# Dense products of a two-block model on one core: one plain fp32 matmul in place of three fp32r matmuls of high and low parts

## The chip, the cores and the metric

One Trainium2 chip, of which the kernel uses one core. The time is microseconds on the device for one execution. Three runs of the kernel before gave 1518.33, 1518.96 and 1520.04 us, a median of 1518.96.

## What is computed

256 tokens of width 1024 go through two blocks in float32. Block 1 has a mixer (gated linear attention beside retention) and a mixture of 32 experts with two experts a token. Block 2 has two layers: a gated recurrence, then a feed-forward; latent attention, then a second feed-forward. Cut to the dense products, it is:

```python
proj = u @ w_in                                   # 1024 -> 11280, split into q, k, v and gates
y_a, y_b = o_gla @ w_br_gla, o_ret @ w_br_ret
h = h + (sigmoid(mga) * y_a + sigmoid(mgb) * y_b) @ w_out
h = h + moe(rmsnorm(h))                           # 32 experts, 1024 -> 512 -> 1024
h = h + hgrn(rmsnorm(h))                          # 1024 -> 4096, recurrence, 1024 -> 1024
h = h + ffn(rmsnorm(h))                           # 1024 -> 2 x 2816, 3-tap convolution, 2816 -> 1024
h = h + mla(rmsnorm(h))                           # 1024 -> 576 latents -> q, k, v; softmax; 1024 -> 1024
h = h + ffn(rmsnorm(h))
```

All weights are float32, 353 pieces of at most 1 MB each.

## The kernel before

Activations stand feature-major (features on partitions, 256 tokens along the free axis) where they are the operand of a product, and token-major elsewhere. Weights come in slots: tiles of 128 x 2048 float32 in a pool of NS = 20, which large activations share. One ordered stream of loads runs on SP's queue (_load, line 302). plan_loads (line 190) goes through a dry run of the program, counts live slots, and so fixes at which points (prefetch) the next loads are issued; a load then waits on SP until its slot's last readers are done, and everything later on SP waits behind it.

A weight other than an expert's is not used as loaded. _split_to (line 311) makes two more slots of it, in four parts each: ACT copies the slot to the format fp32r (high part, tile wh, line 324), and DVE subtracts that from the weight (low part, tile wl, line 325). It runs one weight ahead of the product, two in parts of the attention. Activations are split as well: after a transpose, high_low (line 458) writes xh on ACT and xl on DVE; a feed-forward's hidden tile g is split into hh and hl.

Each product of the dense layers then is three fp32r matmuls (mm3, lines 357 to 361):

```python
mm(out, lh, rh, start=first, stop=False)
mm(out, lh, rl, start=False, stop=False)
mm(out, ll, rh, start=False, stop=last)
```

Names on TensorE: gf is gemm_feat (a weight's 128 x 128 tile stands in the array, 256 tokens stream by), gt is gemm_tok (128 x 128 of the activation stands, 512 weight columns stream by, 288 in the attention's first product), op is out_proj, br the retention branch's product, u and acc the feed-forward's two products (256 and 512 columns), gd a 16-feature product. The experts (gu, y, cb, xg), the retention core (rs, ro), the recurrences' scores (sc, sd, o) and the attention's scores use plain fp32 matmuls on float32 tiles, before and after.

Between the dense products, tick() puts pieces of side work (fillers: decay levels on DVE, scores on TensorE, evacuations on ACT) into the program. The decay levels (tile lv, line 541) are a chain on DVE of eight steps of three operations. In a feed-forward two hidden tiles (u) are followed by the second product (acc) of an earlier pair of them.

Of the kernel before, what the change touches and what calls it, by code (L numbers as in the profile page):

```python
# [12 lines left out]
F32R = mybir.dt.float32r  # L13
# [6 lines left out]
P = 128  # L20
# [10 lines left out]
# 1 / 10000 ** linspace(0, 1, 128) and 10000 ** (-arange(0, 64, 2) / 64), in float32 as the reference rounds them  # L31
# [17 lines left out]
# ---------------------------------------------------------------- host: constants of the shapes  # L49
# [32 lines left out]
# ---------------------------------------------------------------- host: layout of the inputs  # L82
# [79 lines left out]
NS = 20  # L162
# [3 lines left out]
class _Null:  # L166
    """Stands in for the chip while the life of the tiles is counted."""
# [22 lines left out]
def plan_loads(events):  # L190
    """The points of the program at which each weight slot is loaded: as early as the slots allow."""
# [31 lines left out]
class Kern:  # L223
    BUFS = {"t512": 5, "t384": 3, "t256": 7, "t128": 7}

    def __init__(self, ctx, tc, A, coff, poff, upto=None):
# [19 lines left out]
        self.spl = {}  # L246
        self.nsplit = 0
        self.ahead = 1
# [3 lines left out]
    # ---- tiles  # L252
# [37 lines left out]
    # ---- weights: one ordered stream of slots  # L290
    def add(self, key, ap, split):
        self.pos[key] = len(self.stream)
        self.stream.append((key, ap, split))
# [8 lines left out]
    def _load(self):  # L302
        key, ap, split = self.stream[self.loaded]
        t = self.S("w")
        w = ap.shape[-1]
        self.nc.sync.dma_start(t[:, :w], ap)
        self.raw[key] = (t, w)
        self.loaded += 1
        self.events.append("L")

    def _split_to(self, i):
        while self.nsplit <= i and self.nsplit < len(self.stream):
            key, ap, split = self.stream[self.nsplit]
            if not split:
                break
            if self.loaded <= self.nsplit:
                self._load()
            r, w = self.raw.pop(key)
# [7 lines left out]
            self.free(r)  # L326
            self.spl[key] = (h, l)
            self.nsplit += 1

    def get(self, key):  # L330
        i = self.pos[key]
        if self.stream[i][2]:
            self._split_to(i + self.ahead)
            self.prefetch()
            return self.spl.pop(key)
        while self.loaded <= i:
            self._load()
        self.nsplit = max(self.nsplit, i + 1)
        self.prefetch()
        return self.raw.pop(key)[0]  # L340

    # ---- work that runs beside the main products
# [13 lines left out]
    # ---- products  # L356
    def mm3(self, out, lh, ll, rh, rl, first, last):
        mm = self.nc.tensor.matmul
        mm(out, lh, rh, start=first, stop=False)  # L359
        mm(out, lh, rl, start=False, stop=False)  # L360
        mm(out, ll, rh, start=False, stop=last)  # L361

    def gemm_tok(self, keys, xs, evac, kk=4, n=512, ticks=0):
        """[tokens, n] = x @ W; xs(k) -> (high, low, column of the k tile)."""
# [3 lines left out]
        for key in keys:  # L368
            h, l = self.get(key)
            for q in range(kk):  # L370
                xh, xl, o = xs(k)
                for t in range(2):
                    a = slice(o + t * P, o + (t + 1) * P)
                    self.mm3(outs[t][:, :n], xh[:, a], xl[:, a], h[:, q * n:(q + 1) * n], l[:, q * n:(q + 1) * n],
                             k == 0, k == nk - 1)
                k += 1
                if q < kk - 1:
                    self.tick((q + 1) * ticks // kk - q * ticks // kk)
            self.free(h, l)
            self.tick(ticks - (kk - 1) * ticks // kk)  # L380
        evac(outs)

    def gemm_feat(self, keys, xs, evac, kk=4, ticks=0):
        """[512 features, tokens] = W.T @ x.T, two feature tiles a bank."""
# [3 lines left out]
        for key in keys:  # L388
            h, l = self.get(key)
            for q in range(kk):  # L390
                xh, xl, o = xs(k)
                a = slice(o, o + T)
                for ft in range(4):
                    b = slice(q * 512 + ft * P, q * 512 + (ft + 1) * P)
                    self.mm3(outs[ft // 2][:, (ft % 2) * T:(ft % 2 + 1) * T], h[:, b], l[:, b], xh[:, a], xl[:, a],
                             k == 0 and ft % 2 == 0, k == nk - 1 and ft % 2 == 1)
# [3 lines left out]
            self.free(h, l)  # L400
# [3 lines left out]
    def out_proj(self, name, xs, done, mid=None, ticks=0):  # L404
        """x += a @ W, by halves of k, so that the second half of a may come late; done(c): chunk c of x is final."""
        outs = [[self.bank("op") for _ in range(2)] for _ in range(2)]
        for kh in range(2):
            if kh and mid:
                mid()
            for c in range(2):  # L410
                h, l = self.get((name, 2 * kh + c))
                for q in range(4):
                    xh, xl, o = xs(4 * kh + q)
                    for t in range(2):
                        a = slice(o + t * P, o + (t + 1) * P)
                        w = slice(q * 512, (q + 1) * 512)
                        self.mm3(outs[c][t], xh[:, a], xl[:, a], h[:, w], l[:, w], kh == 0 and q == 0,
                                 kh == 1 and q == 3)
                self.free(h, l)
# [7 lines left out]
    # ---- normalisation  # L427
# [22 lines left out]
    def norm_open(self, full=False):  # L450
        n = {"ss": self.small(4, "nss"), "sq": []}
        if full:
            n["f"] = self.S("xf")
        else:
            n["h"], n["l"] = self.S("xh", F32R), self.S("xl", F32R)
        return n

    def high_low(self, b, s, h, l, o):
        a = slice(o, o + T)
        self.nc.scalar.activation(h[:, a], b[:, :T], AF.Copy, scale=s)  # L460
        if l is not None:
            self.nc.vector.scalar_tensor_tensor(l[:, a], b[:, :T], s, h[:, a].bitcast(F32), op0=ALU.mult,
                                                op1=ALU.subtract)

    def norm_chunk(self, n, c, src, wcol):
        """Columns 512 c.. of src [tokens]: transposed, times the weight, split; and their square sums."""
        nc = self.nc
        for k in range(4 * c, 4 * c + 4):
# [3 lines left out]
            self.high_low(b, wcol(k), n.get("h", n.get("f")), n.get("l"), k * T)  # L472
# [18 lines left out]
    def row_of(self, rs):  # L491
        """[128, 256]: the tokens' factors along the free axis, on every partition."""
# [8 lines left out]
    def xs(self, n):  # L501
        return lambda k: (n["h"], n["l"], k * T)

    def transpose_hl(self, src, nk, scale, dst):
        """src(k, t) -> [128 tok, 128]; scale(k) -> [128, 1]; dst(k) -> (high, low, column)."""
        for k in range(nk):
# [3 lines left out]
            self.high_low(b, scale(k), *dst(k))  # L510
# [14 lines left out]
    def decay_levels(self, fr, kq, lv):  # L525
        """[128, 512 + 512] (2 heads x 256 tokens, feature-major) each: products behind | decays (used up); k | q."""
# [23 lines left out]
    def decay_scores(self, lv, kq, h):  # L550
        """Score tiles of one head: SBUF [128, 384] = S^T(0,0) | S^T(0,1) | S^T(1,1)."""
# [42 lines left out]
    def decay_out(self, lv, kq, v, h0, dv):  # L594
        """Both heads of a group: rmsnorm of the output (its weight comes later) in place of v."""
# [44 lines left out]
    # ---------------------------------------------------------------- the program  # L640
# [5 lines left out]
    def setup(self):  # L646
# [14 lines left out]
        for i in range(44):  # L661
            self.add(("in", i), A["w_in"][i], True)
        for n, order in (("br_gla", range(4)), ("br_ret", (0, 4, 1, 5, 2, 6, 3, 7)), ("w_out", range(4))):
            for i in order:
                self.add((n, i), A[n][i], True)
        for e in range(NE):
            for i in range(4):
                self.add(("gu", e, i), A["ex_gu"][e, i], False)
            for i in range(2):
                self.add(("ed", e, i), A["ex_d"][e, i], False)  # L670
        for n, m in (("hg_in", 16), ("hg_out", 4)):
            for i in range(m):
                self.add((n, i), A[n][i], True)

        def ffn(l):
            for kind, i in self.ffn_order():
                if kind == "up":
                    self.add(("f_up", l, i), A["f_up"][l * 22 + i], True)
                else:
                    self.add(("f_dn", l, i), A["f_dn"][l * 11 + i], True)  # L680

        ffn(0)
        for n, o, m in (("ml_in", 0, 4), ("ml_kv", 0, 2), ("ml_q", 0, 3), ("ml_kv", 2, 2), ("ml_out", 0, 4)):
            for i in range(o, o + m):
                self.add((n, i), A[n][i], True)
        ffn(1)

    def slack(self, phase):
        """Slots that the loads leave free for what the phase itself needs next."""
        self.events.append(("slack", SLACK.get(phase, 2)))  # L690

    # ---- block 1, mixer
    def block1_mixer(self):
# [52 lines left out]
        gh, gl = self.small(128, "t128", F32R), self.small(128, "t128", F32R)  # L746
        self.pin(nc.scalar.copy(gh, wgd))
        nc.vector.tensor_sub(gl, wgd, gh.bitcast(F32))
# [970 lines left out]
```

## Time and profile before

| | |
|---|---|
| runs | 1518.33, 1518.96, 1520.04 us |
| profiled execution, first to last instruction (span) | 1516.6 us |
| instructions in it | 24847 |
| bytes read from HBM | 367.24 MB |
| mean granted TensorE clock, share of full | 0.986 |
| weight loads | 353, of 1024 KB or less |

The profiled execution's own time is known as its span; the median of the three runs lies 2.4 us above it. PE stands for TensorE's matmuls, PEld for its weight loads, DVE for VectorE, ACT for ScalarE, POOL for GpSimd and SP for the engine that issues the loads. The length that the trace gives for a matmul contains its way through the array, so consecutive matmuls overlap; the distance between two starts is what one takes of the engine. A busy share of PE is therefore read beside the starts. The granted clock has two levels, 2.4 GHz and 1.2 GHz, shown as 1.00 and 0.50 of full; a mean in between says how long the lower one was given.

### The profile page before, as it was taken

The numbers are of one execution on the slowest core, as the hardware profiler recorded it, in microseconds if no ns is written. First come the engines' busy times: TensorE is split into PE (matmuls) and PEld (weight loads), VectorE is DVE, ScalarE is ACT, GpSimd is POOL, SyncE is SP. The second block draws the span as 40 slices with busy tenths as digits, with TensorE's granted clock in tenths as the row PEclk, the third lists the DMA queues.
The fourth block names the chain that finished last, engine by engine and source line by source line (L and its number), as shares of the span: only waits on it lengthen the run. The fifth ranks groups of instructions, "written<-read, shape, count | busy, mean of one in ns | idle before, by whom it ended". The sixth has DMA issues, their size and how long they took to land. (4 is left out here: it accounts for less than half of the span.)

```text
span 1516.6 us, 24847 instructions
## 1 busy us (share of the span) xinstructions
PE 1435.2 (95%) x10158; PEld 1061.3 (70%) x10158; DVE 792.6 (52%) x1738; ACT 624.9 (41%) x1374; POOL 26.5 (2%) x31
## 2 busy tenths in 40 slices
PE   7999999999899988989989899999999998999998
PEld 7898878877743333333333298779999986799997
DVE  5987475655400000000000079878777767687794
ACT  5645444644200000000000085466656676565672
POOL 0000000000000000000000000000000001000000
PEclk9999999999899999999999999899999999999999
DMA  8335432586799999999999923456554214565500
GB/s 355 130 112 210 179 138 87 201 323 235 295 418 421 421 421 420 420 421 421 421 421 421 408 69 124 152 223 226 191 174 140 72 54 194 200 220 195 192 1 29
DMA packets 53529, 369.96 MB, mean 244 GB/s; under 512 B 6161, under 2 KB 7057, under 8 KB 9634
## 3 DMA queue, kind: packets, MB, share of 16 engines
q1 hardware_dynamic: 53410, 368.31, 62.1%
q8 instruction: 82, 1.34, 0.3%
q14 instruction: 37, 0.30, 0.1%
HBM read 367.24 MB, written 1.05 MB: 243 GB/s over the span
## 5 line engine op out<-in xcount | busy, mean ns | idle before, releaser
L325 DVE TENSOR_TENSOR wl<-w,wh 128x512 fp32r<-128x512 f32 (+2 forms) x644 | 403.9, 666 | 75.1 <-ACT wh L324 56.5
L324 ACT ACTIVATE wh<-w 128x512 fp32r<-128x512 f32 (+2 forms) x644 | 347.8, 613 | 158.6 <-PE u L360 65.8
L1207 PE MATMUL y<-w,t 128*32 128x512 f32 x512 | 227.4, 597 | 10.7 <-ACT t L1200 10.7
L359 PE MATMUL u<-xh,wh 128*128 128x256 f32 x704 | 199.4, 283 | 0.0
L360 PE MATMUL u<-xl,wh 128*128 128x256 f32 x704 | 199.2, 283 | 0.0
L361 PE MATMUL u<-xh,wl 128*128 128x256 f32 x704 | 199.1, 283 | 0.0
L1197 DVE TENSOR_TENSOR t<-t,gu 128x128 f32<-128x128 f32 x32 | 9.2, 288 | 315.5 <-ACT t L1196 315.5
L1207 PEld LDWEIGHTS y<-w,t 128*32 128x32 f32 x512 | 53.9, 110 | 160.7 <-issue 143.3
L1193 PE MATMUL gu<-w,t 128*32 128x256 f32 x2048 | 144.4, 382 | 0.0
L359 PE MATMUL gt<-wh,xh 128*128 128x512 f32 (+1 forms) x352 | 139.4, 396 | 0.0
L359 PEld LDWEIGHTS u<-xh,wh 128*128 128x128 f32 x704 | 134.9, 192 | 0.9
L360 PEld LDWEIGHTS u<-xl,wh 128*128 128x128 f32 x704 | 134.9, 192 | 0.8
L360 PE MATMUL gt<-wl,xh 128*128 128x512 f32 (+1 forms) x352 | 135.2, 384 | 0.0
L361 PE MATMUL gt<-wh,xl 128*128 128x512 f32 (+1 forms) x352 | 135.2, 384 | 0.0
L361 PEld LDWEIGHTS u<-xh,wl 128*128 128x128 f32 x704 | 134.9, 192 | 0.0
L1196 ACT ACTIVATE t<-gu 128x128 f32<-128x128 f32 x32 | 8.9, 278 | 252.2 <-PE gu L1193 252.2
L1193 PEld LDWEIGHTS gu<-w,t 128*32 128x32 f32 x2048 | 68.9, 109 | 56.9 <-issue 20.2
L359 PE MATMUL gf<-xh,wh 128*128 128x256 f32 x320 | 93.4, 292 | 1.7 <-ACT wh L324 1.7
L360 PE MATMUL gf<-xl,wh 128*128 128x256 f32 x320 | 91.9, 287 | 0.0
L361 PE MATMUL gf<-xh,wl 128*128 128x256 f32 x320 | 91.5, 287 | 0.0
L359 PEld LDWEIGHTS gt<-wh,xh 128*128 128x128 f32 x352 | 66.8, 190 | 12.8 <-ACT wh L324 0.5
L360 PEld LDWEIGHTS gt<-wl,xh 128*128 128x128 f32 x352 | 66.8, 190 | 12.9 <-issue 1.0
(394 smaller groups left out, 2144.8 us busy)
## 6 DMA issues: line engine op xcount, KB each, us to landing
w<-in_ex_gu SPq DMA_DIRECT2D x128, 1024.0 KB, 19.0
w<-in_ex_d SPq DMA_DIRECT2D x64, 1024.0 KB, 19.6
w<-in_w_in SPq DMA_DIRECT2D x44, 1024.0 KB, 5.4
w<-in_f_up SPq DMA_DIRECT2D x44, 1024.0 KB, 4.9
w<-in_f_dn SPq DMA_DIRECT2D x22, 1024.0 KB, 4.8
w<-in_hg_in SPq DMA_DIRECT2D x16, 1024.0 KB, 15.7
w<-in_br_ret SPq DMA_DIRECT2D x8, 1024.0 KB, 6.4
w<-in_br_gla SPq DMA_DIRECT2D x4, 1024.0 KB, 5.5
```

The lines of the kernel that those rows point to most:

```text
L324: self.nc.scalar.activation(h[:, a], r[:, a], AF.Copy)
L325: self.nc.vector.tensor_sub(l[:, a], r[:, a], h[:, a].bitcast(F32))
L359: mm(out, lh, rh, start=first, stop=False)
L360: mm(out, lh, rl, start=False, stop=False)
L361: mm(out, ll, rh, start=False, stop=last)
L1193: nc.tensor.matmul(b[32 * j:32 * j + 32, 0:256], xg[k // 4][:, (k % 4) * P + 32 * e:(k % 4) * P + 32 * e + 32], w[:, o:o + 256], start=k = ...
L1196: nc.scalar.activation(sg, b[:, 0:128], AF.Silu)
L1197: nc.vector.tensor_mul(hd, sg, b[:, 128:256])
L1207: self.nc.tensor.matmul(ys[c][32 * e:32 * e + 32, :], hT[:, 32 * j:32 * j + 32], ed[j // 2][:, o:o + 512], start=j == 0, stop=j == 3)
```

## The change

mm3, _split_to and high_low go. Every dense product becomes one plain fp32 matmul on the weight's slot as it was loaded and on one float32 activation tile. A transposed activation is evacuated by one engine (scaled: DVE for odd tiles, ACT for even ones). A weight has one slot instead of two, activations one slot instead of two (xf, oT, rT, mT, cT), and NS is 21. The split of the hidden tile goes, so does the 16-feature weight's. The order of the loads, the experts, the fillers and their ticks stay.

```diff
-NS = 20
+NS = 21
...
-    def _split_to(self, i):
-        while self.nsplit <= i and self.nsplit < len(self.stream):
...
-            h = self.S("wh", F32R)
-            l = self.S("wl", F32R)
-            parts = 4
-            for q in range(parts):
-                a = slice(q * w // parts, (q + 1) * w // parts)
-                self.nc.scalar.activation(h[:, a], r[:, a], AF.Copy)
-                self.nc.vector.tensor_sub(l[:, a], r[:, a], h[:, a].bitcast(F32))
...
     def get(self, key):
...
+        while self.loaded <= self.pos[key]:
             self._load()
         self.prefetch()
+        return self.raw.pop(key)
...
-    def mm3(self, out, lh, ll, rh, rl, first, last):
...
     def gemm_tok(self, keys, xs, evac, kk=4, n=512, ticks=0):
...
-            h, l = self.get(key)
+            w = self.get(key)
             for q in range(kk):
-                xh, xl, o = xs(k)
+                x, o = xs(k)
                 for t in range(2):
-                    a = slice(o + t * P, o + (t + 1) * P)
-                    self.mm3(outs[t][:, :n], xh[:, a], xl[:, a], h[:, q * n:(q + 1) * n], l[:, q * n:(q + 1) * n],
-                             k == 0, k == nk - 1)
+                    self.nc.tensor.matmul(outs[t][:, :n], x[:, o + t * P:o + (t + 1) * P], w[:, q * n:(q + 1) * n],
+                                          start=k == 0, stop=k == nk - 1)
...
-    def high_low(self, b, s, h, l, o):
-        a = slice(o, o + T)
-        self.nc.scalar.activation(h[:, a], b[:, :T], AF.Copy, scale=s)
-        if l is not None:
-            self.nc.vector.scalar_tensor_tensor(l[:, a], b[:, :T], s, h[:, a].bitcast(F32), op0=ALU.mult,
-                                                op1=ALU.subtract)
+    def scaled(self, dst, src, s, k):
+        if k % 2:
+            self.nc.vector.tensor_scalar(dst, src, s, None, op0=ALU.mult)
+        else:
+            self.nc.scalar.activation(dst, src, AF.Copy, scale=s)
...
             for k in range(8):
                 a = slice(k * T, (k + 1) * T)
                 for s in range(2):
-                    w = slice(k * 256 + s * P, k * 256 + (s + 1) * P)
-                    self.mm3(b[:, s * T:(s + 1) * T], h[:, w], lo[:, w], xH[:, a], xL[:, a], k == 0 and s == 0,
-                             k == 7 and s == 1)
+                    nc.tensor.matmul(b[:, s * T:(s + 1) * T], wu[:, k * 256 + s * P:k * 256 + (s + 1) * P], xT[:, a],
+                                     start=k == 0 and s == 0, stop=k == 7 and s == 1)
...
-            nc.scalar.activation(hh, g, AF.Copy)
-            nc.vector.tensor_sub(hl, g, hh.bitcast(F32))
-            hid[f] = (hh, hl)
+            hid[f] = g
```

gemm_feat, out_proj, the retention branch, the feed-forward's second product and the 16-feature product change in the same way.

How instructions stand, at three places. First TensorE in the first feed-forward, where the first hidden tile u begins; before, three matmuls a product, on the high and low parts of the activation and the weight:

```order
L361 MATMUL u_8299<-xh_8199,wl_8222 128x256
L359 MATMUL u_8299<-xh_8199,wh_8221 128x256
L360 MATMUL u_8299<-xl_8200,wh_8221 128x256
L361 MATMUL u_8299<-xh_8199,wl_8222 128x256
L359 MATMUL u_8299<-xh_8199,wh_8221 128x256
L360 MATMUL u_8299<-xl_8200,wh_8221 128x256
L361 MATMUL u_8299<-xh_8199,wl_8222 128x256
L359 MATMUL u_8299<-xh_8199,wh_8221 128x256
L360 MATMUL u_8299<-xl_8200,wh_8221 128x256
```

The same place after, where equal rows follow each other and are counted (x16 is a whole hidden tile):

```order
L1349 MATMUL u_5795<-xf_5744,w_5199 128x256 x15
L451 MATMUL rw_5832<-ident,rsr_5830 128x128 x2
L1349 MATMUL u_5851<-xf_5744,w_5201 128x256 x16
L1349 MATMUL u_5882<-xf_5744,w_5203 128x256 x16
L1376 MATMUL acc_5787<-w_5412,t_1027_5846 128x512
L1376 MATMUL acc_5789<-w_5412,t_1027_5846 128x512
L1376 MATMUL acc_5788<-w_5412,t_1027_5846 128x512
```

Every product now is one instruction; the sequence of u and acc is the same.

Second, DVE in the gated recurrence, at the first decay levels of a group (lv; hfr holds the decays). Before:

```order
L325 TENSOR_TENSOR wl_6700<-w_5914,wh_6699 128x512 x3
L541 TENSOR_TENSOR lv_6716<-hkq_6376,hfr_6375 128x512
L325 TENSOR_TENSOR wl_6748<-w_5916,wh_6747 128x512
L545 TENSOR_TENSOR hfr_6375<-hfr_6375 128x256
L325 TENSOR_TENSOR wl_6748<-w_5916,wh_6747 128x512
L546 TENSOR_TENSOR hfr_6375<-hfr_6375 128x256
L325 TENSOR_TENSOR wl_6748<-w_5916,wh_6747 128x512
L541 TENSOR_TENSOR lv_6716<-hkq_6376,hfr_6375 128x512
```

After:

```order
L1257 TENSOR_TENSOR hkq_4560<-hkq_4560,hfr_4559 128x2x512
L498 TENSOR_TENSOR lv_4708<-hkq_4560,hfr_4559 128x512
L502 TENSOR_TENSOR hfr_4559<-hfr_4559 128x256
L503 TENSOR_TENSOR hfr_4559<-hfr_4559 128x256
L498 TENSOR_TENSOR lv_4708<-hkq_4560,hfr_4559 128x512
```

The weights' subtractions have gone from between the steps of the chain.

Third, ACT in the latent attention, at the evacuation of the keys (kn) from their product's banks. Before:

```order
L1522 COPY kn_10675<-gt_10686 128x512
L1524 ACTIVATE t_1489_10723<-gt_10686 128x512
L1522 COPY kn_10675<-gt_10687 128x512
L1524 ACTIVATE t_1490_10727<-gt_10687 128x512
L324 ACTIVATE wh_10732<-w_10109 128x256 x4
L1522 COPY kn_10675<-gt_10730 128x512
L1524 ACTIVATE t_1495_10755<-gt_10730 128x512
```

After:

```order
L1464 COPY kn_6771<-gt_6782 128x512
L1466 ACTIVATE t_1200_6789<-gt_6782 128x512
L1464 COPY kn_6771<-gt_6783 128x512
L1466 ACTIVATE t_1201_6793<-gt_6783 128x512
L1464 COPY kn_6771<-gt_6796 128x512
L1466 ACTIVATE t_1205_6805<-gt_6796 128x512
```

Here the copies to the high part have gone from between the evacuations.

## Rows read from the trace of the kernel before

**Rows 1.** The page: busy us, share of the span and instructions of each engine.

```profile
PE 1435.2 (95%) x10158; PEld 1061.3 (70%) x10158; DVE 792.6 (52%) x1738; ACT 624.9 (41%) x1374; POOL 26.5 (2%) x31
```

**Rows 2.** Stretches: length; PE, PEld, DVE, ACT, POOL busy (instructions); clock, DMA share, GB/s.

```profile
0.00:380.00 380.00, 368.51 (x2298) 311.94 (x2299) 247.60 (x500) 188.62 (x375) 8.46 (x14) 1.00 0.53 198
380.00:872.00 492.00, 443.56 (x3054) 188.73 (x3052) 45.72 (x161) 41.10 (x113) 0.70 (x1) 0.99 0.99 410
872.00:1026.00 154.00, 145.14 (x1635) 127.90 (x1636) 127.77 (x272) 91.28 (x226) 8.12 (x10) 0.94 0.39 140
1026.00:1222.00 196.00, 195.90 (x1367) 182.61 (x1367) 154.59 (x310) 119.38 (x243) 0.70 (x1) 1.00 0.45 157
1222.00:1326.00 104.00, 95.57 (x506) 75.98 (x504) 70.62 (x207) 74.39 (x203) 7.86 (x4) 0.97 0.41 155
1326.00:1516.60 190.60, 186.52 (x1307) 174.14 (x1306) 146.29 (x292) 110.08 (x218) 0.70 (x1) 1.00 0.37 129
```

**Rows 3.** Timeline of PE, first feed-forward: start us, us, engine, line, operation, tiles.

```profile
1103.72 0.39 PE L359 MATMUL acc<-wh,t 128*128 128x512 f32 x1
...
1107.22 0.28 PE L359 MATMUL u<-xh,wh 128*128 128x256 f32 x1
...
1111.77 0.28 PE L361 MATMUL u<-xh,wl 128*128 128x256 f32 x1
```

**Rows 4.** Timeline of PE in the mixer, at the retention core.

```profile
175.76 1.02 PE L955 MATMUL rs<-rqT,rkT 128*128 128x256 f32 x4
176.62 0.61 PE L958 MATMUL rs<-rqT,rkT 128*128 128x128 f32 x4
...
177.30 0.40 PE L360 MATMUL gt<-wl,xh 128*128 128x512 f32 x1
...
182.10 0.39 PE L360 MATMUL gt<-wl,xh 128*128 128x512 f32 x1
...
182.56 1.02 PE L965 MATMUL ro<-rv,t 128*128 128x512 f32 x2
...
184.28 1.02 PE L967 MATMUL ro<-rv,t 128*128 128x512 f32 x2
```

**Rows 5.** Groups on PE and PEld: tiles, count | busy us, mean ns | idle before.

```profile
L359 PE MATMUL u<-xh,wh 128*128 128x256 f32 x704 | 199.4, 283 | 0.0
L359 PE MATMUL gt<-wh,xh 128*128 128x512 f32 x320 | 129.8, 406 | 0.0
L1217 PE MATMUL cb<-t,t 128*128 128x512 f32 x64 | 29.6, 605 | 0.0
L361 PEld LDWEIGHTS u<-xh,wl 128*128 128x128 f32 x704 | 134.9, 192 | 0.0
```

**Rows 6.** Groups of the split on DVE and ACT, whole span.

```profile
L325 DVE TENSOR_TENSOR wl<-w,wh 128x512 fp32r<-128x512 f32 (+2 forms) x644 | 403.9, 666 | 75.1 <-ACT wh L324 56.5
L324 ACT ACTIVATE wh<-w 128x512 fp32r<-128x512 f32 (+2 forms) x644 | 347.8, 613 | 158.6 <-PE u L360 65.8
```

**Rows 7.** Waits of PE in the mixer, 0 to 380 us: us, times, longest.

```profile
PE gf L359 <- ACT wh L324: 1.7, 1, 1.7
PE gt L360 <- DVE wl L325: 1.2, 1, 1.2
```

**Rows 8.** Waits of PE in the gated recurrence, 872 to 1026 us.

```profile
PE sd L565 <- DVE lv L541: 4.2, 4, 2.1
PE tp L471 <- PEq L1119: 4.1, 1, 4.1
```

**Rows 9.** Groups on DVE in the gated recurrence, 872 to 1026 us.

```profile
L325 DVE TENSOR_TENSOR wl<-w,wh 128x512 fp32r<-128x512 f32 x80 | 52.6, 683 | 1.0 <-ACT wh L324 1.0
```

**Rows 10.** Waits of PE in the latent attention, 1222 to 1326 us.

```profile
PE gt L360 <- DVE wl L325: 3.9, 4, 2.3
PE tp L1553 <- DVE kn L1561: 2.5, 1, 2.5
```

**Rows 11.** Waits of PE in the experts, 380 to 872 us.

```profile
PE gu L1198 <- DMA w<-in_ex_gu: 1.6, 2, 0.8
```

More of the change, by code (lines that the diff above doesn't have):

```diff
@@ L302, in _load @@
     def _load(self):
-        key, ap, split = self.stream[self.loaded]
+        key, ap = self.stream[self.loaded]
         t = self.S("w")
@@ L354, in drain @@
             self.tick()
-    def mm3(self, out, lh, ll, rh, rl, first, last):
[L358 to L361, printed above, removed]
     def gemm_tok(self, keys, xs, evac, kk=4, n=512, ticks=0):
@@ L410, in out_proj @@
             for c in range(2):
-                h, l = self.get((name, 2 * kh + c))
+                w = self.get((name, 2 * kh + c))
                 for q in range(4):
-                    xh, xl, o = xs(4 * kh + q)
+                    xt, o = xs(4 * kh + q)
                     for t in range(2):
[L415 to L419, printed above, removed]
+                        self.nc.tensor.matmul(outs[c][t], xt[:, o + t * P:o + (t + 1) * P],
+                                              w[:, q * 512:(q + 1) * 512], start=kh == 0 and q == 0,
+                                              stop=kh == 1 and q == 3)
+                self.free(w)
                 self.tick(ticks)
@@ L501, in xs, with transposed @@
     def xs(self, n):
-        return lambda k: (n["h"], n["l"], k * T)
-    def transpose_hl(self, src, nk, scale, dst):
+        return lambda k: (n["x"], k * T)
+    def transposed(self, src, nk, scale, dst):
         for k in range(nk):
@@ L751, in block1_mixer @@
             a = slice(k * T, (k + 1) * T)
-            self.mm3(b[0:16, :T], gh[:, k * 16:(k + 1) * 16], gl[:, k * 16:(k + 1) * 16], n["h"][:, a], n["l"][:, a],
-                     k == 0, k == 7)
+            nc.tensor.matmul(b[0:16, :T], wgd[:, k * 16:(k + 1) * 16], n["x"][:, a], start=k == 0, stop=k == 7)
         gd17 = self.small(256, "t256", rows=17)
@@ L906, in block1_mixer @@
         for i in range(2):
-            self.gemm_tok([("br_gla", 2 * i + j) for j in range(2)], lambda k: (oH, oL, k * T), ev_a(i))
-        self.free(oH, oL)
+            self.gemm_tok([("br_gla", 2 * i + j) for j in range(2)], lambda k: (oT, k * T), ev_a(i))
+        self.free(oT)
         outs = [[self.bank("br") for _ in range(2)] for _ in range(2)]
@@ L920, in block1_mixer @@
                     for t in range(2):
-                        a = slice(o + t * P, o + (t + 1) * P)
-                        w = slice(q * 512, (q + 1) * 512)
-                        self.mm3(outs[c][t], xh[:, a], xl[:, a], h[:, w], l[:, w], j == 0 and q == 0,
-                                 j == 3 and q == 3)
-                self.free(h, l)
+                        nc.tensor.matmul(outs[c][t], xr[:, o + t * P:o + (t + 1) * P], w[:, q * 512:(q + 1) * 512],
+                                         start=j == 0 and q == 0, stop=j == 3 and q == 3)
+                self.free(w)
                 if j == 3:
@@ L930, in block1_mixer @@
                         nc.vector.tensor_add(mer[:, a], mer[:, a], mg[1][:, a])
-                    self.now(self.transpose_hl(
+                    self.now(self.transposed(
                         lambda k, t: mer[:, t * D + (4 * c + k) * P:t * D + (4 * c + k + 1) * P], 4, lambda k: 1.0,
-                        lambda k: (mH, mL, (4 * c + k) * T)))
+                        lambda k: (mT, (4 * c + k) * T)))
             if j % 2:
-                self.free(xh, xl)
+                self.free(xr)
         self.free(*mg)
@@ L1431, in down @@
                     for t in range(2):
-                        a = slice(t * P, (t + 1) * P)
                         w = slice(q * 1024 + c * 512, q * 1024 + (c + 1) * 512)
-                        self.mm3(acc[2 * t + c], hs[q][0][:, a], hs[q][1][:, a], h[:, w], lo[:, w],
-                                 i == 0 and q == 0, i == 10 and q == 1)
-            self.free(h, lo)
+                        nc.tensor.matmul(acc[2 * t + c], hs[q][:, t * P:(t + 1) * P], wd[:, w],
+                                         start=i == 0 and q == 0, stop=i == 10 and q == 1)
+            self.free(wd)
         for kind, i in self.ffn_order():
             (up if kind == "up" else down)(i)
-        self.free(xH, xL)
+        self.free(xT)
         nm = self.p("nmix2")
```

156 lines of the change are left out of this document (59 added, 97 removed).

## The prediction

> **What bounds the kernel now.** I read the engines' shares first, then busy time by stretch, then the start times of matmuls, and last the waits. The shares give TensorE (PE) 95% of the span, VectorE (DVE) 52%, ScalarE (ACT) 41% [rows 1]. A busy PE can still be a badly fed one, so the stretches come next [rows 2]. I cut the span at 380, 872, 1026, 1222 and 1326 us: block 1's mixer, the experts, the gated recurrence (HGRN), the first feed-forward, latent attention, the second feed-forward. PE stands idle 0.1 us in the first feed-forward's 196, about 4 in the second's 191 and 11.5 in the mixer's 380. Only HGRN (8.9 idle of 154, mean granted clock 0.94, DVE busy 127.8) and attention (8.4 of 104, clock 0.97) show anything that a relieved DVE or ACT could give back. So the change is decided by what one product costs PE.
>
> A matmul's shown length is no price, since matmuls overlap: u lasts 283 ns [rows 5] but starts every 120 ns. I price by distance of starts. In the feed-forward 38 starts lie between 1107.22 and 1111.77, 120 ns each, and 15 between 1103.72 and 1107.22, 233 ns each at 512 columns [rows 3]; in the mixer 21 starts from 177.30 to 182.10 give 229 ns [rows 4]. Those are the fp32r prices, and each product has three.
>
> Plain fp32 already runs in the same stretch, on 128x128 weights, in the retention core. The trace shows every plain fp32 matmul as two records. Four records of rs (256 columns) take 175.76 to 176.62, 215 ns each; four of ro (512 columns) take 182.56 to 184.28, 430 ns each [rows 4]. The mean of cb, 605 against gt's 406 for the same shape, tells the same of 64 more records [rows 5].
>
> **The change, priced.** Product of 256 columns: 3 x 120 = 359 ns becomes 2 x 215 = 430, +71. Product of 512 columns: 3 x 229 = 686 becomes 2 x 430 = 860, +174; in acc, which pays 233 now, 3 x 233 = 700 becomes 860, +160. For the 32 products of 288 columns I scale the first by width, +80. The clock is at its upper level where I took these.
>
> Products come from the loops of the code, and the counts of the groups agree where they are shown (u 704, gt 320) [rows 5].
> - Mixer: 192 gf and 8 gd of 256 columns, +14.2 us; 256 gt, 32 gt on oh, 64 br and 32 op of 512, 384 in all, +66.8. Together +81.0.
> - Experts: already plain fp32, untouched.
> - HGRN: 128 gf, +9.1; 64 gt and 32 op, +16.7. Together +25.8.
> - Each feed-forward: 352 u, +25.0; 88 acc, +14.1. Both together +78.2.
> - Attention: 28 gt on the latents and 32 op, +10.4; 32 of 288 columns, +2.6. Together +13.0.
>
> All of it is 198 us, if PE is always the last to be ready.
>
> What comes off the other engines: 644 subtractions (403.9 us of DVE) and 644 copies (347.8 us of ACT) [rows 6], half the evacuations of transposed activations (now one engine each, by turns, where before ACT and then DVE did every one), and the split of the hidden tiles. In both feed-forwards that is worth nothing, since PE waits there for neither. Elsewhere I take back only named waits and lost clock:
> - Mixer: the first product's wait for wh, 1.7 us, and one for wl, 1.2 [rows 7]. -3.
> - HGRN: 8.9 us idle, of which 4.1 is the branch behind the experts and stays [rows 8]. Most of the other 4.8 is scores waiting for DVE's decay levels (4.2) [rows 8], and DVE gets 52.6 of its 127.8 us back [rows 2, 9]. The clock of 0.94 costs 0.06 x 154 = 9.2 us, which denser PE work should win back. Together -14. Bounds: nothing back, or all 25.8, as PE then still has that work to do.
> - Attention: the wait for wl, 3.9 us, goes, and the one for kn, 2.5, shrinks with ACT's four-part copies gone from between the evacuations [rows 10]; with some clock (0.03 x 104 = 3 us) I take -8. Bounds 0 and -11.5, all idle time and lost clock.
>
> The remaining edits cost nothing. The loads keep their number and order on SP's queue and gain lead (one slot a weight instead of two behind the split, 21 slots for 20). What hides them is that a 1.05 MB load takes 2.6 us at 410 GB/s [rows 2] and a slot now feeds PE for 6.9 us (16 products of 430 ns, or 8 of 860); without that cover each late load would cost up to 2.6 us. The decay table's load, now behind more weight loads on SP, is first used near 176 us. Nothing moves on POOL. Nothing new waits: a product waits for its load instead of for a split of it.
>
> Sum: mixer 78, HGRN 12, feed-forwards 78, attention 5, which is **+173 us**. The profiled span of 1516.6 becomes 1690; the median of the runs, 1518.96, is 2.4 above that span, so I forecast **1692**.
>
> **A rule weighed against rows.** A group's weight loads last 192 ns in u [rows 5] while u starts every 120 ns [rows 3], so a load runs beside the matmul before it, and the number of loads sets no time. The Trainium skill (TensorE: Matmul & The Clock Gate, part 3, The mechanism) says that a weight load overlaps matmuls in flight only when its row group differs. All dense products here use all rows, so by that rule the loads would stand in line, which is the third rival below. The trace disagrees: a start every 120 ns has no room for a 192 ns load in line. By the row the sum is +173, by the rule it would be a gain.
>
> **The rivals.**
> - *Nothing comes back.* The freed DVE and ACT time is worth nothing because PE's stalls in HGRN and attention are dependencies that merely move. For it: DVE's levels are a chain of steps. Against: its wl subtractions stand between those steps now. +198, **1717**.
> - *Dense plain fp32 has the surplus that fp32r has.* From 120 and 229 ns, an fp32r matmul costs 109 for 256 columns and 11 more, while plain records show 215 and 430 with none [rows 3, 4]. If those 11 ns came from dense switching of weights and not from the format, 1780 x 2 records would pay them too: 39 us on 1692, **1731**. Against: rs switches weights at every record too.
> - *The other side: weight loads set the pace.* Then the drop from three loads a product to two is what counts: 1780 x 192 ns = 342 us gained against 198 lost, **1375**. It decides as soon as over 111 ns of a load (198/1780) stand uncovered. For it: the weight-load row is busy 70% of the span [rows 1]. Against: 192 does not fit into 120.
> - *The expert stage was bound by its loads.* DMA is at 0.99 there [rows 2]. Then five more loads ahead (the four slots of two split weights, and the one added) would save about 5 x 2.6 = 13 us: **1679**. Against: PE waits 1.6 us for those loads in all [rows 11], so the two are only near each other.
> - *The change doesn't do what it says*, a product still being issued as several. The order on PE shows one instruction a product, so this is left only within the chance of no change.
>
> **How the numbers follow.** The forecast has 0.75, for 1672 to 1710 (HGRN from +1 to +26, attention from +1 to +13, the mixer 4 less to 3 more). Nothing back: 0.09. The surplus: 0.06. The expert stage: 0.06, inside the same range. The weight loads: 0.03. No change: 0.01. I take the range from 1665, the forecast's low end with part of the experts' 13 us, to 1722, past the case with nothing back; that leaves out the surplus, the weight loads and the outer ends, under 0.2. About 0.2% (3 us) can be told from no change by a measurement. Faster by more than that is the weight-load case alone, 0.03; within it 0.01; slower 0.96.
>
> **What would show it.** Right: plain u records start every 215 ns and acc and gt every 430; the two feed-forwards take about 39 us more each and are full of PE; the experts keep their 490 us or so; HGRN has a granted clock nearer 1 and fewer waits for lv. Wrong in size: record distances of 226 and 441, or HGRN 25 us longer with its waits in place. Wrong altogether: record distances of about 120 and 230, or a feed-forward shorter than 196 us.

## The result and the profile after

Four runs of the changed kernel gave 1687.62 to 1689.66 us, a median of **1688.67**, beside 1518.64 for the kernel before on the same chip (1518.04 to 1520.04): a ratio of 1.112 [1.1104, 1.1136] (in brackets, here and below, the 95% interval). The forecast was 1692, range 1665 to 1722. Slower came, by 170 us where 173 was forecast.

The page of the changed kernel, busy time of each engine, then the granted clock in 40 slices and three groups:

```profile
PE 1622.0 (96%) x8378; PEld 939.8 (56%) x8378; DVE 409.4 (24%) x1003; ACT 263.8 (16%) x639; POOL 24.1 (1%) x31
...
PEclk9999999999989999999999999999999999999999
...
L1349 PE MATMUL u<-xf,w 128*128 128x256 f32 x1408 | 307.8, 379 | 0.0
...
L1349 PEld LDWEIGHTS u<-xf,w 128*128 128x128 f32 x1408 | 267.1, 190 | 43.7 <-issue 8.6
...
L1376 PE MATMUL acc<-w,t 128*128 128x512 f32 x352 | 154.3, 592 | 0.0
```

Against [rows 1], DVE lost 383 us of work and ACT 361; PE gained 187 and sets the time. There are 1780 matmul records and 1780 weight loads fewer (10158 to 8378), and the kernel is slower. 704 products u show as 1408 records: two a product.

The timeline of PE after, in the second feed-forward (start us, us, engine, line, operation, tiles, count):

```profile
1483.68 13.98 PE L1349 MATMUL u<-xf,w 128*128 128x256 f32 x64
1497.49 7.03 PE L1376 MATMUL acc<-w,t 128*128 128x512 f32 x16
1504.36 1.89 PE L1349 MATMUL u<-xf,w 128*128 128x256 f32 x8
```

64 records of u take 13.81 us, 216 ns each, and 16 of acc 6.87, 429 each, as rs and ro did before [rows 4].

Now the stretches. The prediction's cuts do not fall on the same work in two kernels, so from here on all are cut at work: the mixer ends at the first matmul of the router, the experts with HGRN's first transposes, HGRN at the first u, each feed-forward at its last acc or first u. After (length; PE, PEld, DVE, ACT, POOL busy; clock, DMA share, GB/s):

```profile
0.00:472.00 472.00, 464.57 (x1794) 255.11 (x1795) 108.94 (x250) 59.97 (x126) 7.17 (x14) 1.00 0.47 177
472.00:952.00 480.00, 429.01 (x2993) 177.90 (x2992) 41.83 (x157) 36.53 (x103) 0.70 (x1) 0.98 0.99 410
952.00:1121.70 169.70, 168.68 (x1424) 110.52 (x1423) 81.45 (x185) 46.94 (x136) 7.36 (x10) 0.99 0.41 155
1121.70:1350.00 228.30, 228.30 (x890) 167.93 (x889) 69.30 (x144) 36.82 (x77) 0.69 (x1) 1.00 0.36 123
1350.00:1455.20 105.20, 102.85 (x397) 60.53 (x396) 37.74 (x127) 45.44 (x121) 7.50 (x4) 1.00 0.42 160
```

Before, the three stretches that gave something back, with the same cuts (mixer, HGRN, attention):

```profile
0.00:396.80 396.80, 385.21 (x2378) 325.58 (x2378) 254.03 (x509) 194.36 (x389) 8.46 (x14) 1.00 0.54 203
877.40:1032.10 154.70, 147.85 (x1651) 129.37 (x1649) 131.00 (x278) 94.47 (x233) 8.12 (x10) 0.96 0.38 139
1221.00:1323.30 102.30, 93.87 (x491) 74.19 (x489) 68.90 (x203) 72.08 (x194) 7.86 (x4) 0.97 0.39 150
```

Cut exactly at those matmuls (the table's last row is the price of the products less the measured difference):

| us | mixer | experts | HGRN | 1st feed-forward | attention | 2nd feed-forward |
|---|---|---|---|---|---|---|
| before | 396.8 | 480.6 | 154.7 | 188.9 | 102.3 | 188.9 |
| after | 471.9 | 479.7 | 170.1 | 227.9 | 105.6 | 227.9 |
| difference | +75.1 | -0.9 | +15.4 | +39.0 | +3.3 | +39.0 |
| price of the products | +81.0 | 0 | +25.8 | +39.1 | +13.0 | +39.1 |
| came back | 5.9 | 0.9 | 10.4 | 0.1 | 9.7 | 0.1 |

The waits of PE after: in the mixer (0 to 472 us), then in HGRN (952 to 1122), then in attention (1350 to 1455.2); us, times, longest:

```profile
PE tp L465 <- DVE mga L881: 0.7, 1, 0.7
PE gf L357 <- DVE xf L417: 0.6, 1, 0.6
```

```profile
PE sc L519 <- issue: 0.6, 1, 0.6
PE op L378 <- ACT oT L419: 0.4, 1, 0.4
```

```profile
PE tp L1494 <- DVE rope L1508: 1.3, 1, 1.3
...
PE tp L1494 <- DVE kn L1502: 0.5, 1, 0.5
```

The waits for wl and wh are gone [rows 7, 10], for lv too [rows 8], and kn's fell from 2.5 to 0.5 us. What is new is small: 1.3 us for rope in attention and 0.6 for the first xf.

### The profile page after: what moved, and what is told of

The parts are those of the page before. It is cut to its first block, busy times and chain, and to the rows that moved or that the text cites. A ratio compares the mean times of both kernels' runs of the same rounds, so it can differ in the third digit from the quotient of the medians.

```text
span 1687.8 us, 19722 instructions
## 1 busy us (share of the span) xinstructions
PE 1622.0 (96%) x8378; PEld 939.8 (56%) x8378; DVE 409.4 (24%) x1003; ACT 263.8 (16%) x639; POOL 24.1 (1%) x31
## 5 line engine op out<-in xcount | busy, mean ns | idle before, releaser
L1349 PE MATMUL u<-xf,w 128*128 128x256 f32 x1408 | 307.8, 379 | 0.0
L338 PE MATMUL gt<-w,xf 128*128 128x512 f32 (+1 forms) x704 | 295.7, 575 | 0.0
L1349 PEld LDWEIGHTS u<-xf,w 128*128 128x128 f32 x1408 | 267.1, 190 | 43.7 <-issue 8.6
L338 PEld LDWEIGHTS gt<-w,xf 128*128 128x128 f32 x704 | 131.8, 190 | 143.9 <-issue 137.8
L1376 PE MATMUL acc<-w,t 128*128 128x512 f32 x352 | 154.3, 592 | 0.0
L357 PE MATMUL gf<-xf,w 128*128 128x256 f32 x640 | 144.2, 384 | 0.6 <-DVE xf L417 0.6
L357 PEld LDWEIGHTS gf<-xf,w 128*128 128x128 f32 x640 | 122.0, 193 | 19.3 <-issue 1.8
L1376 PEld LDWEIGHTS acc<-w,t 128*128 128x128 f32 x352 | 66.9, 190 | 75.7 <-issue 68.4
L1362 DVE SCALAR_TENSOR_TENSOR t<-t,prm,t 128x255 f32<-128x255 f32 (+1 forms) x176 | 81.2, 482 | 32.5 <-ACT t L1360 29.4
L378 PE MATMUL op<-w,oT 128*128 128x512 f32 x128 | 56.5, 594 | 0.4 <-ACT oT L419 0.4
```

What stands on the lines that cost most here:

```text
L338: self.nc.tensor.matmul(outs[t][:, :n], x[:, o + t * P:o + (t + 1) * P], w[:, q * n:(q + 1) * n], start=k == 0, stop=k == nk - 1)
L357: self.nc.tensor.matmul(outs[ft // 2][:, (ft % 2) * T:(ft % 2 + 1) * T], w[:, q * 512 + ft * P:q * 512 + (ft + 1) * P], x[:, o:o + T], sta ...
L378: self.nc.tensor.matmul(outs[c][t], xt[:, o + t * P:o + (t + 1) * P], w[:, q * 512:(q + 1) * 512], start=kh == 0 and q == 0, stop=kh == 1 ...
L1349: nc.tensor.matmul(b[:, s * T:(s + 1) * T], wu[:, k * 256 + s * P:k * 256 + (s + 1) * P], xT[:, a], start=k == 0 and s == 0, stop=k == 7 a ...
L1362: nc.vector.scalar_tensor_tensor(ys[:, j:], us[:, :T - j], cw[:, 3 * c + 2 - j:3 * c + 3 - j], ys[:, j:], op0=ALU.mult, op1=ALU.add)
L1376: nc.tensor.matmul(acc[2 * t + c], hs[q][:, t * P:(t + 1) * P], wd[:, w], start=i == 0 and q == 0, stop=i == 10 and q == 1)
```

## The experiments

A stage's length is read from one profile. In the four kernels here that leave HGRN as it was it took 154.7 to 159.5 us, where the kernel before took 154.7, so a difference of less than 5 us there, read from one profile alone, says little; mixers with the same code lie between 395.4 and 397.9, the other stages within about 1.

**The change in the feed-forwards only** (the kernel before elsewhere), to see whether the terms of the sum add up (u shown; acc, the activation tile and the hidden tile change with it):

```diff
-                    self.add(("f_up", l, i), A["f_up"][l * 22 + i], True)
+                    self.add(("f_up", l, i), A["f_up"][l * 22 + i], False)
...
-                    self.mm3(b[:, s * T:(s + 1) * T], h[:, w], lo[:, w], xH[:, a], xL[:, a], k == 0 and s == 0,
-                             k == 7 and s == 1)
+                    nc.tensor.matmul(b[:, s * T:(s + 1) * T], wu[:, w], xT[:, a], start=k == 0 and s == 0,
+                                     stop=k == 7 and s == 1)
```

> The kernel before with the change made in the two feed-forwards alone. It tells whether the terms of the sum add up stage by stage. Theory (each stage pays its own products): each feed-forward 189 to 228 us, all else as before, 1518.6 + 78 = 1597, within 3 us. Rival (the freed slots and engines help the stages beside it, so that a part has less effect than its share of the whole): 1590 or less.

1597.52 us, ratio 1.0528 [1.051, 1.0546], +79 us. The first feed-forward's stretch:

```profile
1032.40:1259.90 227.50, 227.50 (x885) 167.47 (x884) 68.97 (x145) 38.76 (x83) 0.70 (x1) 1.00 0.32 116
```

No idle time, full clock, 38.6 us longer; the second gained 39.0. The terms add up stage by stage.

**The split kept, its results unread.** Everything as changed, but ACT and DVE still split each dense weight, into small scrap tiles (the activations' split stays away; 19 slots, to make room). It keeps the long products and takes the relief away.

```diff
-NS = 21
+NS = 19
...
+                self.nc.scalar.activation(h, r[:, a], AF.Copy)
+                self.nc.vector.tensor_sub(l, r[:, a], h.bitcast(F32))
...
+        if key[0] not in ("gu", "ed"):
+            self._split(i)
+            self._split(i + 1)
```

> The changed kernel, but every dense weight is still split into a high and a low part by ACT and DVE, into scrap tiles that nothing reads (19 slots, the scrap takes the other two). Products run plain on the weights as loaded. It tells apart why the gated recurrence and the attention grew by less than their products. Theory (DVE and ACT time freed by the split is what came back): the 10.3 us of the recurrence, about 6 of the attention's 9.8 and some 3 of the mixer's 5.9 are lost again, 1688.7 + 19 = 1708, with waits of PE for decay levels back and the recurrence's granted clock under 0.97. Rival (the idle time went only because longer products leave the side work more time): 1689, within 3 us, clock of the recurrence 0.99 as it is.

1750.21 us, ratio 1.1523 [1.1504, 1.1542]. Two new waits of PE spoil it, in the mixer and ahead of HGRN:

```profile
PE gf L377 <- ACT xf L439: 38.5, 1, 38.5
...
PE tp L447 <- DVEq L1090: 21.3, 1, 21.3
```

The scheduler had put copies of later weights ahead of the first evacuations on ACT: 47 of them ran from 10.0 us on before the first xf (ACT's timeline, the longest run of copies and that evacuation):

```profile
26.22 12.14 ACT L320 ACTIVATE wh<-w 128x512 fp32r<-128x512 f32 x20 [0.40 <-DVE wl L321]
...
47.55 1.55 ACT L439 ACTIVATE xf<-tp,prm 128x256 f32<-128x256 f32 x4
```

DVE's branch behind the experts came late as well (4.1 us in the other kernels [rows 8]). Less 38.5 and 17.2 it would be 1694.5: mixer and experts as in the changed kernel, HGRN 3.5 us longer, attention 2.2. So it does not read as a price of the split, and was mended.

**The split kept, its place pinned.** The same, with the first weight left out and each split held at its place in program order (against the run above):

```diff
-                self.nc.scalar.activation(h, r[:, a], AF.Copy)
-                self.nc.vector.tensor_sub(l, r[:, a], h.bitcast(F32))
+                self.pin(self.nc.scalar.activation(h, r[:, a], AF.Copy))
+                self.pin(self.nc.vector.tensor_sub(l, r[:, a], h.bitcast(F32)))
```

> The run with the split kept, mended: there ACT had taken splits ahead of the first evacuation (TensorE waited 38.5 us for it) and ahead of the branch behind the experts (21.3 us instead of 4.1). Here the first weight is not split and every split stands where the program asks for it. Without those two waits that run would have had 1750.2 - 38.5 - 17.2 = 1694.5, with the recurrence 3.5 us and the attention 2.2 us longer than in the changed kernel and the mixer as long. Theory now (of what came back, DVE's and ACT's freed time gave about 6 us, the rest came with the products themselves, which wait for no split and leave the side work more time): 1694.5, 1692 to 1698. Rival (the first theory: all of it is freed time): 1708.

1712.86 us, ratio 1.1292 [1.1273, 1.1311]. Neither expectation is met by its own places, though the total is near one. Mixer, HGRN and attention:

```profile
0.00:470.90 470.90, 461.90 (x1792) 253.04 (x1793) 250.95 (x486) 187.65 (x361) 7.19 (x14) 1.00 0.46 173
952.00:1123.90 171.90, 168.16 (x1426) 109.70 (x1425) 130.13 (x270) 91.52 (x221) 7.37 (x10) 1.00 0.41 152
1352.90:1474.90 122.00, 112.68 (x399) 65.19 (x398) 63.68 (x187) 67.85 (x181) 7.51 (x4) 0.90 0.37 138
```

In the mixer DVE has 142 us of work more than in the changed kernel and ACT 128, and the stage is 1 us shorter. In HGRN DVE has 49 more and ACT 45, and it is 1.8 us longer. Attention is 16.5 us longer: 7 of it is idle time, and the clock of 0.90, which on 122 us is 12 lost at most, is left for the other 9.5. In it the largest wait is one for ACT; ACT's timeline ahead of it and the stretches around it follow:

```profile
PE s L1612 <- ACT ropeT L1516: 5.0, 1, 5.0
```

```profile
1408.98 2.19 ACT L320 ACTIVATE wh<-w 128x512 fp32r<-128x512 f32 x4 [2.93 <-DVE wl L321]
1411.07 1.25 ACT L1516 ACTIVATE qT<-tp,prm 128x512 f32<-128x512 f32 x2
1412.21 1.08 ACT L1516 ACTIVATE ropeT<-tp 128x512 f32<-128x512 f32 x2
```

```profile
1410.00:1415.00 5.00, 2.14 (x6) 1.27 (x8) 2.36 (x4) 3.29 (x7) 0.00 (x0) 0.75 1.00 383
1415.00:1430.00 15.00, 13.94 (x37) 7.31 (x38) 5.98 (x27) 6.42 (x19) 0.00 (x0) 0.50 0.20 83
```

Four pinned copies stood ahead of the evacuations and had themselves waited 2.93 us for DVE's subtractions (presumably for the four buffers of their scrap tile; not shown). Behind PE's wait the clock was 0.50 for at least 15 us. So the 16.5 us cannot be read as a price of the split.

**HGRN without its splits, short products kept.** The kernel before, but in HGRN the first weight's parts serve for all 20 weights; the other 19 weights are left out of the computation.

```diff
+            if key[0] in ("hg_in", "hg_out") and key != ("hg_in", 0):
+                self.free(r)
+                self.spl[key] = self.one
+                self.nsplit += 1
+                continue
```

> The kernel before, in the gated recurrence alone without any split: its first weight's two parts stand for all 20 weights there (which are loaded and left out of the products), so the products keep three fp32r matmuls and their length, while ACT's 76 copies and DVE's 76 subtractions of that stage are gone, and TensorE waits for no weight. All else as before. It closes the question of what came back in the recurrence. Theory (the side work's own chain leaves TensorE its gaps with short products; the change's longer products filled them, the freed engines did not): the recurrence 151 to 155 us against 154.7, 1516 +- 3. Rival (the freed time of both engines together was what came back): 145 or less there, 1508 or less.

1511.82 us, ratio 0.9947 [0.993, 0.9963], 7 us faster. HGRN's stretch and PE's largest wait in it:

```profile
877.60:1026.20 148.60, 145.08 (x1650) 127.15 (x1649) 90.18 (x202) 55.63 (x157) 7.56 (x10) 0.98 0.34 133
```

```profile
PE sd L576 <- DVE lv L552: 2.4, 2, 1.3
```

6.1 us less, between the two expectations; the runs' own 7 us, 5.6 to 10.6 by the interval, bear it out. The decay levels are still waited for, 2.4 us where it was 4.2 [rows 8]. With the splits their slots go too, which this run does not tell apart.

**DVE alone relieved.** The kernel before with a tile of zeros as every weight's low part; the low parts of the weights are left out, the number of matmuls stays.

```diff
-            l = self.S("wl", F32R)
+            l = self.zero
...
-                self.nc.vector.tensor_sub(l[:, a], r[:, a], h[:, a].bitcast(F32))
```

> The kernel before with three fp32r matmuls a product, ACT's copies kept, but the low parts of the weights left out: a tile of zeros stands for wl, so DVE's 644 subtractions (403.9 us) and TensorE's waits for them are gone while the products keep their length. Theory (with short products DVE's time does matter in the recurrence, where it is busy 127.8 of 154 us, and the waits for wl are real): recurrence 154.7 to about 145, attention 102.3 to 97, mixer 396.8 to 394, feed-forwards 189 as they are, 1518.6 - 18 = 1500. Rival (freed time is worth nothing, the side work's own chain sets the waits): 1518.6 less the waits for wl of 5 us, 1513.

1510.5 us, ratio 0.9952 [0.9936, 0.9969]. HGRN's stretch:

```profile
875.50:1029.20 153.70, 147.95 (x1650) 129.90 (x1649) 86.15 (x194) 94.23 (x232) 7.56 (x10) 0.96 0.40 146
```

DVE fell from 131.0 to 86.2 us, and the stage by 1.0. Idle time is 5.8 us for 6.9, and the clock stays. Attention:

```profile
1218.70:1316.60 97.90, 90.22 (x489) 72.93 (x488) 44.34 (x143) 71.73 (x194) 7.50 (x4) 0.98 0.40 153
```

It fell by 4.3, near the 3.9 us that PE waited for wl there [rows 10], but the wait for kn grew from 2.5 to 4.4, and the idle time shown fell by 0.7 only (8.4 to 7.7); the rest of the 4.3 is traced in part only, by a clock of 0.98 for 0.97. The rival's 1513 is nearer than the theory's 1500. That a matmul on zeros draws the same clock as one on the low part is taken for granted here.

**Plain products on the latents only.** The kernel before with the change for the 28 gt of attention on the latents, among which the waits for wl stand (the two calls for keys shown; those for q and v change in the same way):

```diff
-            self.gemm_tok([("ml_kv", i)], lambda k: (cH, cL, k * T), ev_k(i), kk=2)
+            self.gemm_plain([("ml_kv", i)], lambda k: (cT, k * T), ev_k(i), kk=2)
```

> The kernel before with plain fp32 in the attention's seven products on the latents alone (28 of the 60 wide products there), whose weights are no longer split. Theory (what came back in the attention are the waits on ACT's and DVE's splits between the evacuations): TensorE pays 28 x 0.174 = 4.9 us more and gets back most of 9.8, so 1518.6 - 4 = 1515, with no wait for wl left. Rival (nothing comes back, the stall is the chain of norms and only moves): 1518.6 + 4.9 = 1523.5.

1514.6 us, ratio 0.9981 [0.9967, 0.9995], 4 us faster. Attention's stretch:

```profile
1219.20:1318.50 99.30, 93.79 (x463) 66.83 (x461) 59.21 (x171) 64.00 (x166) 7.51 (x4) 1.00 0.40 149
```

The clock went from 0.97 to 1.00. The products cost 28 x 174 ns = 4.9 us and the stage fell by 3.0, so 7.9 came back.

**Fourteen slots.** The changed kernel with less lead for the loads:

```diff
-NS = 21
+NS = 14
```

> The changed kernel with 14 slots in place of 21. It tests the slots and the rival that the experts are bound by their loads. Theory (TensorE sets the pace everywhere, loads are only near it in the experts): mixer, recurrence, feed-forwards and attention keep their times within 1 us each; the experts lose 0 to 8 us as seven loads less lie ahead of a stage in which loads need about 0.3 us an expert more than TensorE; 1689 to 1697. Rival (the experts are bound by loads): seven loads less ahead cost 7 x 2.6 = 18 us, 1707, with waits for the experts' loads on PE.

1695.84 us, ratio 1.117 [1.1151, 1.1188], 7.2 above the changed kernel. All of it is in the experts, 8.7 us longer (just past the theory's 8, half of the rival's 18), where PE now waits for a load again:

```profile
PE gu L1144 <- DMA w<-in_ex_gu: 3.2, 3, 1.4
```

That wait is 3.2 of the 8.7 us; the rest is not traced. With 21 slots no wait for a load is left there, and going from 20 with two a weight to 21 with one gave 0.9: with 21 slots PE sets the stage's time, with 14 the loads do in part.

**Three bf16 matmuls in the feed-forwards.** The kernel before with both high and low parts in bf16 there; three matmuls a product as before, parts that hold fewer bits.

```diff
+            half = key[0] in ("f_up", "f_dn")
+            if half:
+                hl = self.S("wb", BF16, 4096)
+                h, l = hl[:, 0:2048], hl[:, 2048:4096]
...
-            nc.vector.tensor_sub(hl, g, hh.bitcast(F32))
+            nc.vector.tensor_sub(hl, g, hh)
```

> The kernel before with the feed-forwards' high and low parts in bf16 instead of fp32r: still three matmuls a product, but high and low part hold fewer bits of each operand together. It measures where the surplus of an fp32r matmul comes from (120 ns between starts for 256 columns, 233 for 512 in acc, where plain fp32 pays 107 and 214 for each of its passes). Theory (the surplus is the format's): starts every 109 and 216 ns, 3 x 704 x 0.011 + 3 x 176 x 0.017 = 32 us less, 1487. Rival (any dense stream of three matmuls a product with changing weights pays it): 1518.6, within 3 us.

1493.2 us, ratio 0.9832 [0.9819, 0.9845], the fastest with the next one. The timeline of PE in the first feed-forward:

```profile
1106.22 0.38 PE L365 MATMUL acc<-wb,t 128*128 128x512 bf16 x1
...
1110.97 0.38 PE L366 MATMUL acc<-wb,t 128*128 128x512 bf16 x1
1111.19 0.27 PE L364 MATMUL u<-xb,wb 128*128 128x256 bf16 x1
...
1118.94 0.27 PE L366 MATMUL u<-xb,wb 128*128 128x256 bf16 x1
```

22 starts of acc take 4.75 us, 216 ns each, and 71 of u take 7.75, 109 each, where fp32r has 233 and 120 [rows 3]. A weight load changed as well, 98 ns where fp32r shows 192 [rows 5]:

```profile
L365 PEld LDWEIGHTS <-wb 128*128 128x128 bf16 x352 | 34.4, 98 | 4.9
```

The stage's stretch, and PE's waits in it:

```profile
1037.80:1215.50 177.70, 173.03 (x1315) 129.11 (x1324) 152.45 (x306) 114.87 (x233) 0.70 (x1) 1.00 0.45 156
```

```profile
PE rw L503 <- DVE rsr L448: 2.6, 1, 2.6
PE u L366 <- DVE wb L330: 1.5, 2, 1.2
```

The matmuls are worth 352 x 33 + 88 x 51 = 16 us a feed-forward; it got 11.2 shorter (13.4 in the second), as PE now stands idle 4.7 us where it never did. So 24.6 us of the expected 32 came, which is why 1487 was expected and 1493 came. (The profiled execution was slower, 1498.0 us from first to last instruction, with 159.5 in HGRN, which this kernel leaves as it was.)

**Both of these together**, the bf16 feed-forwards and the plain latents:

> Two parts together, the bf16 parts of the feed-forwards (1493.2 alone) and the latents' plain products (4.0 us less alone) on the kernel before. If each stage pays its own, 1489; if they share a gain, 1493.

1493.71 us, ratio 0.9849 [0.9824, 0.9874]. Its profile has attention at 99.3 us and feed-forwards of 177.5 and 175.4, so both parts show in their stages, but the medians of 1493.71 and 1493.2 do not show the second. Its four runs lie between 1490.42 and 1497.72, wider than the 4 us in question; why the median kept nothing is open.

## Why the prediction was right, and where its reasons failed

**The price of a product** carried it: start distances of 216 and 429 ns for a forecast of 215 and 430, feed-forwards at +39.0 each for 39.1, and +38.6 and +39.0 when they alone were changed. PE had nothing idle there to give back, so the whole price stayed.

**What came back** in all was 27 us of 198, for 25 forecast (3, 14 and 8). That rules out the 1717 of "nothing comes back". By stage:

- Mixer, 5.9 for 3: idle time fell from 11.6 to 7.4 us. The waits for wh and wl went, with one of 0.6 for xf in their place, and the one for mga, which the forecast left out, fell from 1.9 to 0.7. The clock gave about 1.6 more: before, it fell to 0.89 over 15 us ahead of the last products, after, the stage has 1.00. In two kernels that leave the mixer as it was (latents, feed-forwards only) that fall is missing as well, at 395.4 and 395.5 us for 396.8, so this part may be chance. DVE's and ACT's relief as such is worth nothing that one profile can show here: with their splits back in, the stage takes 470.9 us for 471.9. The fall of the clock:

```profile
365.00:380.00 15.00, 13.08 (x55) 10.49 (x54) 11.18 (x23) 8.52 (x20) 0.00 (x0) 0.89 0.77 307
```

- Attention, 9.7 for 8: idle time fell by 6.1 us (8.4 to 2.4), and the clock of 0.97, worth 3 us, became 1.00. Plain products on the latents alone, with their weights' splits gone, gave 7.9 of it; dropping wl's subtraction alone gave 4.3. So the direct waits for the split, with the clock that fell around them, seem to be most of it; the first of these runs made 28 products longer as well, and does not tell that apart. What the place of ACT's copies adds is open: splits put back cost 2.2 us where the scheduler could place them, and 16.5 where they were pinned.
- HGRN, 10.4 for 14: here is the **step that failed**, in size by its clock and in its reason by DVE. Idle time fell from 6.9 to 1.0 us, 5.9 for the 4.8 forecast. The clock went from 0.96 to 0.99, 6.2 - 1.7 = 4.5 us (two decimals leave this open by 1.6), for the 9.2 forecast. Of those 9.2, about 5.4 x 0.32 = 1.7 lay ahead of HGRN's first product, in the stretch of the branch behind the experts, which the forecast itself had said stays, and it did (before, then after):

```profile
872.00:877.40 5.40, 3.29 (x17) 3.32 (x18) 2.05 (x5) 2.59 (x7) 0.00 (x0) 0.68 0.62 214
946.00:951.60 5.60, 3.45 (x17) 3.48 (x18) 1.46 (x3) 1.61 (x4) 0.00 (x0) 0.61 1.02 423
```

The rest of the miss is rounding, what the lower clock still takes after (1.7), and the spread of the stage. The reason given for the idle time was "DVE gets 52.6 of its 127.8 us back". Four kernels show how far that carries:

| HGRN, us | weights split | not split | difference |
|---|---|---|---|
| three fp32r matmuls | 154.7 | 148.6 | -6.1 |
| one plain matmul | 171.9 | 170.1 | -1.8 |
| difference | +17.2 | +21.5 | |

The products were priced at 25.8. With ACT and DVE loaded with the splits about as before, the stage grows by 17.2 only: in that order the longer products bring 8.6 us of the 10.4 themselves, and relief of both engines adds 1.8 (3.5 by the run with the split not pinned), within what one profile can tell. In the other order relief brings 6.1 and the longer products 4.3. So the two are not a sum: each takes away some of the same idle time and lost clock, and either alone gave more than half of the 10.4. With longer products and the splits kept, PE waits 1.3 us for lv where it waited 4.2 [rows 8], and the clock is 1.00, as the forecast's clause on denser PE work said:

```profile
PE sd L543 <- DVE lv L519: 1.3, 1, 1.3
```

Relief of DVE alone, which the step named, gave 1.0 with short products. Given the spread of 154.7 to 159.5, it is shown that longer products cost less than their price without any relief (17.2 for 25.8), and that relief gains with short products; the share of each is not. So the reason was half right, and that the size came as near as it did is in part luck. The rows before allowed the other reading: PE's own work there was to grow by 25.8 us, well over the idle time and lost clock that it could fill.

**The rivals.** The surplus of fp32r (1731) falls: dense plain fp32 shows none, and bf16, which also changes weights at every matmul, starts every 109 and 216 ns. The 11 ns go with the format; whether with the multiplication or with fp32r's longer weight load (192 ns for 98) no run here tells apart. The expert stage (1679) falls with -0.9 us; fourteen slots show that its loads are near, at 8.7 us for seven slots less. Weight loads as the pace (1375) fall: 1780 fewer, and 170 us slower. The rule of the Trainium skill behind it (TensorE: Matmul & The Clock Gate, part 3, The mechanism: a weight load overlaps matmuls in flight only where its row group differs; the text above that rule also lets a load go ahead into the background weight buffer) does not agree with these traces as the list states it: full-array fp32r matmuls start every 120 ns with a load of 192 ns each, and bf16 ones every 109 with one of 98.

## What to carry to other kernels

Price a matmul by the distance of its starts in a stretch where PE waits for nothing, and count its records: a plain fp32 product is two of 216 ns for 256 columns, an fp32r split three of 120, so the split was shorter on PE (360 for 432 ns), and it won here because ACT and DVE had room for it. Where PE sets the time, work taken off other engines was worth about the waits of PE that name it and the clock lost around them, and longer PE work fills some of those waits too. The fastest form measured here keeps three matmuls and makes the parts bf16 in the feed-forwards, 1493.2 us, if fewer bits will do; then PE begins to wait for DVE.

## What was not expected of the hardware

- An fp32r matmul costs more than a bf16 one of the same size: 120 for 109 ns at 256 columns, 233 for 216 at 512. The surplus grows less than the columns do, 11 and 17 ns. Plain fp32 pays twice the bf16 figure for each of its two records (216 and 429).
- With the split kept and placed by the scheduler, 47 copies on ACT ran ahead of the first evacuation, and PE waited 38.5 us for it. Work whose results nobody reads can cost as much as that by its place alone.
- The granted clock of attention fell to 0.90 in the run with pinned splits, where it was 0.50 for at least 15 us behind PE's wait of 5.0, and rose to 1.00 when 28 products were made plain (0.97 before): in this stage the clock moved the time about as much as the waits did.
